# Moving modulation products from the latent attention's out projection to the even mixer behind it

## The chip, the core and the metric

The kernel runs on one NeuronCore of a Trainium2 chip. The metric is device time in microseconds (us), lower is better. It is the median of three runs, and one further execution was taken with a profiler that records every instruction of every engine. The engines are TensorE (PE, with its weight loads, PEld), VectorE (DVE), ScalarE (ACT), GpSimd (POOL) and SyncE (SP), which issues nearly all DMA transfers, in order, from one queue.

## The reference

Two transformer blocks of two layers each run over 256 latent and 256 context tokens of width 2048, all in float32. The mixers in order are a windowed attention, a latent attention (MLA), an "even" mixer (pooling, and a recurrence in both directions with 16 heads of 64) and an attention with grouped keys. Each layer is modulated by a condition vector:

```python
shift_l, scale_l, gate_l = jnp.split((sc @ mod_w[l] + mod_b[l])[:, None, :], 3, axis=-1)
hl = xl * (1.0 + scale_l) + shift_l
...
xl = layer_norm(DEEPNORM_ALPHA * xl + gate_l * yl, ln_g[l], ln_b[l])
```

`sc @ mod_w[l]` is a product of one row (two with the context's condition) by a 2048 x 6144 matrix. It depends on nothing but the inputs, so its place in the program is free as long as shift, scale and gate are there when a layer asks for them. There are four such matrices, 48 MB (MiB) each.

## The kernel before

Activations lie in SBUF with features on the partitions, as a rounded high part and a low rest (`hhi`, `hlo`). A dense layer streams its weights: `weights` loads two K-tiles (two times 128 rows, 512 columns) per DMA into a tile `raw`, `split` makes a high part `whi` (ACT, L323) and a low part `wlo` (DVE, L324), and PE makes three products for each block (`mm3`, L352 to L354). `weights` calls `fill()` once after each K-tile.

A modulation step (L260, in `mod_steps`) multiplies one 1 MB tile `mraw` of a modulation matrix (four K-tiles of 512 columns) by the condition. It is one row of the program on PE, "32x512 x4", and 8 records in the trace: four products on four column groups of the array. A batch of 16 steps ends with an ACT copy (L267) and four small products (L273). `fill` runs such steps at a rate per K-tile that is set anew for each of six stages by the table `PACE`:

```python
def fill(self):
    if self.mod_wait:
        self.mod_wait -= 1
        if not self.mod_wait and not self.mod_ahead:
            self.mod_load()
    for n in list(self.side):
        self.owed_side[n] = self.owed_side.get(n, 0.0) + self.side[n][1]
        steps = int(self.owed_side[n])
        self.owed_side[n] -= steps
        self.advance(n, steps)
```

`PACE` has the windowed attention, its out projection, the latent attention, its out projection, the even mixer, its out projection. Behind the last there is no modulation left. `mod_open` also gives a stage its number of `mraw` buffers: three in the out projections, one in the three mixers. `mod_load` issues the tile's DMA on SP. `need` runs the remaining steps of a group at once if a layer asks for one that isn't done.

The stage in question (L1757 to L1794) is the latent attention's out projection: four groups of 512 output columns, each of 16 K-tiles with 12 products of 256 columns, then the first weights of the even mixer (`ev_lora`, 2 times 16 K-tiles with 6 products each). A group ends with `residual` (DVE, L1471). Beside groups 1 to 3 and the first `ev_lora` pass run the puts (`put_h`) of the next layer's operands, two ACT and one DVE operation each. At the end the layer's result is stored (`xscratch`, L1793, 4 stores of 1 MB).

The even mixer (`even`, L945) runs 240 K-tiles of weights, with 512-column products, and beside them 16 units of the recurrence, up to four at a time, advanced by `fill` as well: long chains of small products on PE with DVE and ACT between them. `bon` (L1220) is one product of a unit that waits for a DVE operation (L1218). In this mixer `raw` has two buffers.

The order of instructions on each engine is set at build time, by a scheduler that puts instructions in order by when it thinks they are ready. The engines then run their queues in that order.

Of the kernel before, what the change touches and what calls it, by code (L numbers as in the profile page):

```python
# [36 lines left out]
ACTIVE = 4  # L37


PACE = 0.3, 0.5, 0.2, 0.5, 0.25, 0.5  # L40
MV_LAG = 1
MOD_LAG = 2
MEX = 1
# [73 lines left out]
class Net:  # L117
# [552 lines left out]
    def gqa(self, w, windowed, kb, v=None):  # L670
# [5 lines left out]
        with self.tc.tile_pool(name=pre, bufs=1) as ph:  # L676
# [28 lines left out]
            if windowed:  # L705
                self.mod_open(ph, 1, PACE[0])
            toks = range(q0 // P, 4)
# [75 lines left out]
    def mla(self, kvb):  # L783
        nc, I, h = self.nc, self.I, self.h
        scale = 192 ** -0.5
        with self.tc.tile_pool(name="mla", bufs=1) as ph:
# [39 lines left out]
            self.lin_tok(I["mla_in"][0], h, KD, 512, range(2, 4), ev_cq)  # L826
            self.mod_open(ph, 1, PACE[2])
            self.more(ph, MEX, RX[2], 2 * HG * P)
# [116 lines left out]
    def even(self, lb):  # L945
# [3 lines left out]
        with self.tc.tile_pool(name="ev", bufs=1) as ph:  # L949
            self.mod_open(ph, 1, PACE[4])  # L950
            if EX:
# [678 lines left out]
def tile_network(ctx, tc, I, out, dbg=None, stop=9):  # L1630
# [94 lines left out]
    with tc.tile_pool(name="x1", bufs=1) as px:  # L1725
        xn = px.tile([P, KD, NT], F32, name="x1")
        N.more(px, XX[0], RX[1])
        N.mod_open(px, 3, PACE[1])
        N.need(0, range(12))
# [28 lines left out]
    with tc.tile_pool(name="x2", bufs=1) as px:  # L1758
        xn = px.tile([P, KD, NT], F32, name="x2")
        N.more(px, XX[1], RX[3])  # L1760
        N.mod_open(px, 3, PACE[3])
        N.need(1, range(12))
# [37 lines left out]
    with tc.tile_pool(name="x3", bufs=1) as px:  # L1800
        xn = px.tile([P, KD, NT], F32, name="x3")
        N.more(px, XX[2], RX[5])
        N.mod_open(px, 3, PACE[5])
        N.need(2, range(12))
# [195 lines left out]
```

## Time and profile before

| what | value |
|---|---|
| median of 3 runs | 3386.61 us (3378.92 to 3392.72) |
| profiled execution, its own time | 3385.91 us |
| its span, first to last instruction | 3384.1 us |
| TensorE busy | 3198.0 us, 95% |
| weight loads busy (beside PE) | 2384.4 us, 70% |
| VectorE busy | 2051.4 us, 61% |
| ScalarE busy | 1541.6 us, 46% |
| modulation products (L260) busy | 234.0 us, 1536 records, 192 steps |
| mean granted TensorE clock | 0.978 |

PE is the busiest engine nearly everywhere. Busy time of PE counts overlapping products once, and the end of each is modelled, so a busy PE can still have room between the starts of its products. The stage of the change lies between 1356 and 1574 us of the span, the even mixer from there to about 2700, its out projection to about 2900.

### The profile page before, as it was taken

To read this page: it belongs to the slowest core of one execution; us is meant where nothing else is said; L and a number is where in the kernel's file an instruction comes from. 1 tells how busy PE (TensorE), PEld (TensorE's weight loads), DVE (VectorE), ACT (ScalarE), POOL (GpSimd) and SP (SyncE) were. 2 spreads that over 40 slices of the span, in tenths; PEclk is the share of its full clock that TensorE was granted. 3 is DMA by queue.
4 is the path that set the end of the run, shared out by engine and by line. 5 is a ranking of instruction groups with operands and counts; after the bars stand their busy time and mean duration, and the time that the engine had idled before them with its cause. 6 is when DMAs were issued, how large, how long until landed. Compare 5 with 4: busy or idle time off the path is not lost. (4 is left out here: it accounts for less than half of the span.)

```text
span 3384.1 us, 56050 instructions
## 1 busy us (share of the span) xinstructions
PE 3198.0 (95%) x21218; PEld 2384.4 (70%) x21218; DVE 2051.4 (61%) x4487; ACT 1541.6 (46%) x3461; POOL 195.8 (6%) x277
## 2 busy tenths in 40 slices
PE   5999999989989999898999989999999999899998
PEld 2567777767877777665766666666666678778887
DVE  2456455543476666442776676777777655867767
ACT  2424444442366655442344434444444433636654
POOL 0000000000001110000000000000000001200000
PEclk8999999999999999999999999999999999999999
DMA  7843444358654655988534222222323444544454
GB/s 299 307 161 126 144 140 144 131 198 292 213 166 155 212 193 194 369 340 320 170 119 125 76 76 79 73 73 66 99 80 93 133 168 131 174 129 144 132 174 157
DMA packets 270784, 556.27 MB, mean 164 GB/s; under 512 B 122928, under 2 KB 150704, under 8 KB 244912
## 3 DMA queue, kind: packets, MB, share of 16 engines
q1 hardware_dynamic: 270512, 552.68, 49.0%
q8 instruction: 167, 2.74, 0.3%
q14 instruction: 105, 0.86, 0.1%
HBM read 517.46 MB, written 35.13 MB: 163 GB/s over the span
## 5 line engine op out<-in xcount | busy, mean ns | idle before, releaser
L324 DVE TENSOR_TENSOR wlo<-raw,whi 128x512 fp32r<-128x512 f32 (+2 forms) x1000 | 658.7, 668 | 610.4 <-ACT whi L323 573.3
L352 PE MATMUL a<-hhi,whi 128*128 128x512 f32 (+1 forms) x2752 | 975.9, 357 | 32.6 <-ACT whi L323 29.6
L323 ACT CAST whi<-raw 128x512 fp32r<-128x512 f32 (+2 forms) x1000 | 591.8, 599 | 865.1 <-PE a L353 448.9
L353 PE MATMUL a<-hlo,whi 128*128 128x512 f32 (+1 forms) x2752 | 950.5, 347 | 0.2 <-DVE hlo L445 0.2
L354 PE MATMUL a<-hhi,wlo 128*128 128x512 f32 (+1 forms) x2752 | 938.6, 349 | 5.6 <-DVE wlo L324 5.1
L352 PEld LDWEIGHTS a<-hhi,whi 128*128 128x128 f32 x2752 | 524.3, 191 | 192.9 <-ACT whi L323 79.6
L354 PEld LDWEIGHTS a<-hhi,wlo 128*128 128x128 f32 x2752 | 518.5, 191 | 72.5 <-DVE wlo L324 14.1
L353 PEld LDWEIGHTS a<-hlo,whi 128*128 128x128 f32 x2752 | 525.3, 191 | 54.2 <-issue 3.0
L352 PE MATMUL a<-whi,hhi 128*128 128x512 f32 (+1 forms) x672 | 262.8, 401 | 16.1 <-ACT sq L613 5.9
L353 PE MATMUL a<-wlo,hhi 128*128 128x512 f32 (+1 forms) x672 | 264.5, 394 | 0.3
L456 POOL TENSOR_TENSOR rs<-st,mhalf 128x4 f32<-128x4 f32 (+3 forms) x109 | 140.9, 1293 | 2097.5 <-DVE st L453 1910.8
L354 PE MATMUL a<-whi,hlo 128*128 128x512 f32 (+1 forms) x672 | 260.4, 390 | 0.0
L260 PE MATMUL mv<-mraw,cs 128*32 128x512 f32 x1536 | 234.0, 632 | 21.4 <-DMA mraw<-mod_w 21.3
L352 PEld LDWEIGHTS a<-whi,hhi 128*128 128x128 f32 x672 | 127.1, 191 | 74.2 <-issue 22.2
L353 PEld LDWEIGHTS a<-wlo,hhi 128*128 128x128 f32 x672 | 128.9, 192 | 30.0 <-DVE wlo L324 5.4
L354 PEld LDWEIGHTS a<-whi,hlo 128*128 128x128 f32 x672 | 128.9, 192 | 26.0 <-issue 1.1
L565 ACT ACTIVATE pr<-sc,nm 128x512 f32<-128x512 f32 (+1 forms) x128 | 81.0, 632 | 93.3 <-DVE nm L562 62.6
L1385 ACT ACTIVATE SD<-SV,DL 64x64 f32<-64x64 f32 x224 | 77.2, 345 | 63.3 <-DVE SV L1399 60.1
L556 DVE TENSOR_REDUCE mx<-sc 128x1 f32<-128x512 f32 (+1 forms) x128 | 78.9, 617 | 40.3 <-PE sc L354 23.4
L1399 DVE SCALAR_TENSOR_TENSOR SV<-chain,DL,SD 64x64 f32<-64x64 f32 x224 | 63.3, 283 | 59.7 <-PE chain L1393 51.6
L572 ACT ACTIVATE pr<-pr,rc 128x512 f32<-128x512 f32 (+1 forms) x128 | 85.6, 669 | 22.0 <-DVE rc L571 21.9
L260 PEld LDWEIGHTS mv<-mraw,cs 128*32 128x32 f32 x1536 | 33.9, 110 | 85.1 <-issue 38.6
(371 smaller groups left out, 4465.9 us busy)
## 6 DMA issues: line engine op xcount, KB each, us to landing
mraw<-mod_w SPq DMA_DIRECT2D x192, 1024.0 KB, 5.0
raw<-od_in SPq DMA_DIRECT2D x88, 512.0 KB, 3.5
raw<-swa_in SPq DMA_DIRECT2D x72, 512.0 KB, 3.6
raw<-ev_rkv SPq DMA_DIRECT2D x64, 384.0 KB, 3.5
raw<-ev_in SPq DMA_DIRECT2D x48, 512.0 KB, 3.6
raw<-swa_out SPq DMA_DIRECT2D x40, 512.0 KB, 5.6
raw<-ev_out SPq DMA_DIRECT2D x40, 512.0 KB, 3.4
raw<-mla_g SPq DMA_DIRECT2D x64, 256.0 KB, 3.1
```

What stands on the lines that cost most here:

```text
L260: nc.tensor.matmul(pb[32 * j : 32 * j + 32, :], cs[:, 32 * k + 30 - 2 * n : 32 * k + 62 - 2 * n], raw[:, j, :], start=(n == 0 and q == 0), ...
L323: nc.scalar.copy(whi, raw)
L324: nc.vector.tensor_tensor(wlo, raw, whi.bitcast(F32), op=ALU.subtract)
L352: mm(out, ah, bh, start=first, stop=False, skip_group_check=shared)
L353: mm(out, ah, bl, start=False, stop=False, skip_group_check=shared)
L354: mm(out, al, bh, start=False, stop=last, skip_group_check=shared)
L456: self.nc.gpsimd.tensor_tensor(dst, stv, mv, op=ALU.pow)
L556: nc.vector.reduce_max(mx, sc, axis=AX.X)
L565: nc.scalar.activation(pr[:, :n], sc, AF.Exp, scale=scale, bias=nm, accum_out=sm)
L572: nc.scalar.activation(pr[:, :n], pr[:, :n], AF.Copy, scale=rc)
L1385: nc.scalar.activation(SD[r_], SV[r_, hh, c, :], AF.Copy, scale=DL[r_, c : c + 1])
L1399: nc.vector.scalar_tensor_tensor(SV[r_, hh, c + 1, :], ps[r_, 128:192], DL[r_, c : c + 1], SD[r_], ALU.mult, ALU.add)
```

## The change

One number of the table: the rate of modulation steps beside the latent attention's out projection becomes 0.

```diff
-PACE = 0.3, 0.5, 0.2, 0.5, 0.25, 0.5
+PACE = 0.3, 0.5, 0.2, 0, 0.25, 0.5
```

On PE, in group 1 of the projection (a_13503 to a_13506, the accumulators of one group before, a_13455 to a_13458 now), a modulation step stood behind every second K-tile. Before:

```order
L353 MATMUL a_13506<-hlo,whi_13755 128x256
L354 MATMUL a_13506<-hhi,wlo_13756 128x256
L260 MATMUL mv_13896<-mraw_13749,cs_9274 32x512 x4
L352 MATMUL a_13503<-hhi,whi_13777 128x256
L353 MATMUL a_13503<-hlo,whi_13777 128x256
```

and now:

```order
L353 MATMUL a_13458<-hlo,whi_13481 128x256
L354 MATMUL a_13458<-hhi,wlo_13482 128x256
L352 MATMUL a_13455<-hhi,whi_13503 128x256
L353 MATMUL a_13455<-hlo,whi_13503 128x256
L354 MATMUL a_13455<-hhi,wlo_13504 128x256
```

The step is gone and the K-tiles follow each other. In all, 45 of the 192 steps leave this stage, 3 stay at its start.

On SP, at the end of the stage, the last weights of `ev_lora` and the first of the even mixer (`ev_rkv`) stood beside modulation tiles, with the four stores of the result between them. Before:

```order
L240 DMA mraw_14989<-mod_w 128x2048
L338 DMA raw_15001<-ev_lora 128x512
L240 DMA mraw_15013<-mod_w 128x2048
L1793 DMA xscratch<-x_13094 128x2048 x4
L338 DMA raw_15048<-ev_rkv 128x768
L338 DMA raw_15082<-ev_rkv 128x768
L240 DMA mraw_15063<-mod_w 128x2048
```

and now:

```order
L338 DMA raw_14521<-ev_lora 128x512
L1793 DMA xscratch<-x_13094 128x2048
L338 DMA raw_14539<-ev_lora 128x512
...
L338 DMA raw_14701<-ev_lora 128x512
L338 DMA raw_14719<-ev_lora 128x512
L338 DMA raw_14760<-ev_rkv 128x768
L338 DMA raw_14794<-ev_rkv 128x768
L240 DMA mraw_14775<-mod_w 128x2048
```

The last store stands eleven loads ahead of the even mixer's first weights, the three others earlier still, and no modulation tile lies between them.

On PE in the even mixer (the seventh chunk of the recurrence's sixth unit, `chain`), before:

```order
L354 MATMUL a_19495<-hhi,wlo_19915 128x512
L1404 MATMUL chain_19587<-SV_19089,QB_18892 64x64 x2
L352 MATMUL a_19496<-hhi,whi_19914 128x512
L353 MATMUL a_19496<-hlo,whi_19914 128x512
L354 MATMUL a_19496<-hhi,wlo_19915 128x512
L1376 MATMUL chain_19587<-SV_19089,AQ_18678 64x64 x2
```

and now:

```order
L1404 MATMUL chain_19324<-SV_18814,QB_18611 64x64 x2
L353 MATMUL a_19229<-hlo,whi_19728 128x512
L354 MATMUL a_19229<-hhi,wlo_19729 128x512
L260 MATMUL mv_17136<-mraw_19629,cs_9274 32x512
L1376 MATMUL chain_19324<-SV_18814,AQ_18391 64x64 x2
L260 MATMUL mv_17136<-mraw_19629,cs_9274 32x512 x3
```

A modulation step has come in, and the scheduler has cut it in two around a product of the recurrence. The even mixer had 16 steps and 4 such cuts; it now has 51 steps and 22 cuts. Its out projection had no step and has 10, with one cut.

## Rows read from the trace of the kernel before

**Rows 1.** Stretch, its us, busy PE PEld DVE ACT POOL (records), clock, DMA share, GB/s.
```profile
1356.30:1404.80 48.50, 37.76 (x253) 27.26 (x250) 18.63 (x39) 19.49 (x44) 0.00 (x0) 0.86 1.00 379
1404.80:1438.10 33.30, 32.52 (x258) 25.45 (x258) 15.01 (x33) 16.56 (x35) 0.00 (x0) 1.00 0.94 364
1438.10:1471.20 33.10, 33.01 (x251) 24.92 (x251) 12.64 (x23) 11.18 (x22) 0.00 (x0) 1.00 0.96 373
1471.20:1507.50 36.30, 32.89 (x258) 24.70 (x257) 16.88 (x32) 17.58 (x36) 0.00 (x0) 1.00 0.96 360
1507.50:1562.00 54.50, 49.69 (x321) 30.32 (x320) 14.28 (x28) 13.36 (x25) 0.00 (x0) 0.94 0.87 341
1562.00:1573.60 11.60, 1.09 (x10) 0.17 (x9) 1.67 (x6) 1.55 (x4) 1.46 (x13) 0.64 0.92 363
```

**Rows 2.** PE in time order, one period of group 1 (start, length, instruction, count).
```profile
1409.86 1.07 PE L260 MATMUL mv<-mraw,cs 128*32 128x512 f32 x8
...
1413.92 0.64 PE L260 MATMUL mv<-mraw,cs 128*32 128x512 f32 x4
```

**Rows 3.** PE in time order: the last layer's out projection begins.
```profile
3266.09 0.74 PE L352 MATMUL a<-hhi,whi 128*128 128x256 f32 x4 [1.17 <-ACT hhi L444]
```

**Rows 4.** DVE in time order: `residual` ends groups 0 and 1 of that projection.
```profile
3294.92 1.66 DVE L1471 SCALAR_TENSOR_TENSOR x<-a,mod,res 128x256 f32<-128x256 f32 x4 [0.58 <-PE a L354]
...
3318.60 1.66 DVE L1471 SCALAR_TENSOR_TENSOR x<-a,mod,res 128x256 f32<-128x256 f32 x4 [0.58 <-PE a L354]
```

**Rows 5.** ACT by line and form, groups 1 to 3 (1404 to 1507).
```profile
L323 ACT CAST whi<-raw 128x512 fp32r<-128x512 f32 x48 | 27.2, 616 | 32.4 <-DMA raw<-mla_out 23.9 <-PE a L353 4.1 <-PE mv L260 3.2
L494 ACT ACTIVATE hf<-x,mod,s 128x256 f32<-128x256 f32 x22 | 12.6, 598 | 4.6 <-DVE hlo L500 4.6
L498 ACT CAST hhi<-hf 128x256 fp32r<-128x256 f32 x23 | 8.8, 404 | 10.6 <-PE a L354 10.6
```

**Rows 6.** PE's waits, 1560 to 1578 (in total, times, longest).
```profile
PE a L352 <- ACT whi L323: 10.7, 2, 10.5
```

**Rows 7.** Busy time in two stretches of 24 K-tiles each in the even mixer.
```profile
1688.50:1822.30 133.80, 132.63 (x1109) 86.93 (x1108) 92.27 (x211) 56.91 (x154) 9.88 (x21) 1.00 0.37 114
1965.80:2095.30 129.50, 125.51 (x1061) 86.55 (x1060) 92.87 (x212) 56.90 (x155) 9.07 (x17) 0.99 0.27 72
```

**Rows 8.** PE's waits: first in 1688.5 to 1822.3, then in 1965.8 to 2095.3.
```profile
PE bon L1220 <- DVE r L1218: 0.9, 1, 0.9
...
PE bon L1220 <- DVE r L1218: 4.0, 1, 4.0
```

**Rows 9.** PE in time order: a cut step in the even mixer.
```profile
1812.10 1.05 PE L260 MATMUL mv<-mraw,cs 128*32 128x512 f32 x2
1813.07 1.20 PE L354 MATMUL a<-hhi,wlo 128*128 128x512 f32 x4
1814.20 1.06 PE L260 MATMUL mv<-mraw,cs 128*32 128x512 f32 x6
1815.19 0.98 PE L1430 MATMUL yt<-ident,y 128*128 128x128 f32 x7
```

**Rows 10.** Busy time: even mixer without steps, its out projection, the last out projection.
```profile
1890.00:2690.00 800.00, 769.89 (x6491) 526.54 (x6491) 583.44 (x1332) 358.33 (x965) 54.69 (x97) 0.98 0.31 85
2806.00:2850.00 44.00, 44.00 (x196) 36.45 (x195) 20.76 (x35) 12.27 (x20) 5.83 (x4) 1.00 0.35 110
3295.00:3318.00 23.00, 23.00 (x194) 23.00 (x194) 18.97 (x42) 11.58 (x23) 0.00 (x0) 1.00 0.72 221
```

**Rows 11.** PE's waits in the even mixer without steps (1890 to 2690), the longest one.
```profile
PE bon L1220 <- DVE r L1218: 16.2, 6, 5.4
```

**Rows 12.** SP's waits in the even mixer with steps (1600 to 1890).
```profile
SPq L240 <- PE mv L260: 51.9, 10, 11.0
```

**Rows 13.** The page, DMA issues (KB each, us to landing).
```profile
raw<-ev_rkv SPq DMA_DIRECT2D x64, 384.0 KB, 3.5
raw<-mla_out SPq DMA_DIRECT2D x32, 512.0 KB, 8.1
```

## The prediction

> **What bounds the kernel now.** I read the busy time by stretch first, because one share over the whole span mixes stages with different limits. In the six stretches of the stage that changes [rows 1] the DMA engines are busy 87 to 100% of the time and move 341 to 379 GB/s, while TensorE (PE) is busy 38 of 48 us in group 0 and 33 of 36 in group 3. The granted clock is 0.86 in group 0 and 0.64 in the last stretch, that is, a part of each runs at 1.2 GHz, behind the waits, where the rest has 2.4. So the stage has two limits: PE where the products stand close, the DMA engines elsewhere. The same shape of work without modulation is in the trace: the last layer's out projection, whose groups keep PE busy 23.0 of 23.0 us at 221 GB/s and a clock of 1.00 [rows 10]. A weight tile of 512 KB lands 8.1 us after its issue in our stage, where one of 384 KB in the even mixer takes 3.5 [rows 13], and ScalarE (ACT) spends 23.9 us of three groups idle until a weight tile lands [rows 5]. The reader is to see in this that a modulation step costs twice: once on PE, and once as a megabyte that stands before the weights.
>
> The even mixer has the opposite face. Its DMA share is 0.31 and it moves 85 GB/s; PE is busy 770 of 800 us [rows 10]. What PE waits for longest is VectorE (DVE), at the product `bon` of the recurrence: 16.2 us in 6 waits [rows 11].
>
> **The change part by part.** Moved are 45 steps: 35 go to the even mixer, 10 to its out projection.
>
> *A step on PE.* In group 1 two K-tiles and a step take 1413.92 - 1409.86 = 4.06 us [rows 2]. Two K-tiles alone take (3318.60 - 3294.92) / 8 = 2.96 us in the last out projection [rows 4]. A step costs 1.1 us where PE is full.
>
> *What the stage loses.* Groups 1 and 2: from 33.3 and 33.1 us [rows 1] to 23.7 each [rows 4]; ACT has room for it (16 casts at 0.616, 8 puts at 0.598 + 0.404, together 17.9 us [rows 5]). Saved: 9.6 + 9.4 = 19.0.
> Group 0: its twin, also with operands that come back from memory, takes 3294.92 - 3266.09 = 28.8 us [rows 3, 4]. One step stays (1.1), and I add 3 us because that step's tile still has to land before PE goes on: 33, from 48.5. Saved: 15.5 (19.7 if it is as its twin).
> Group 3: 12 of its 16 K-tiles have a put beside them, on ACT 0.616 + 0.598 + 0.404 = 1.6 us against PE's 1.48 a K-tile. So 12 x 1.62 + 4 x 1.48 = 25.3 us; I take 26, from 36.3. Saved: 10.3.
> `ev_lora`: 192 products, as many as a group has, so 23.7 at best; with four puts at its start I take 26, from 54.5. It is the richest stretch because its 32 K-tiles had only 6 products each, and the steps' megabytes stood against so little PE time. Saved: 28.5.
> The wait behind it: PE stands 10.5 us until the even mixer's first weights are converted [rows 6]. Ahead of them in the queue now stand 4 MB of stores and modulation tiles; afterwards one store at most, eleven loads before. I leave 3 of the 11.6 us. Saved: 8.6.
> Together 15.5 + 19.0 + 10.3 + 28.5 + 8.6 = 82 us. From below: if the waits stay and only PE work goes, 45 x 1.1 = 50. From above: group 0 as its twin, group 3 and `ev_lora` at 23.7, no wait: 94.
>
> *What the even mixer pays.* Two of its stretches of 24 K-tiles hold the same instructions, one with modulation steps and one without: 1109 and 1061 PE records, 48 or six steps apart, DVE 211 and 212 [rows 7]. They take 133.8 and 129.5 us. Six steps cost 4.3 us, 0.72 each, two of the six being cut. The saving against the full price lies in `bon`: PE waits 4.0 us there without the steps and 0.9 with them [rows 8], because PE comes later to a VectorE that is behind. Without that, (4.3 + 3.1) / 6 = 1.23 a step. For 35 steps these ends give 25 and 43 us; I take 1.0, 35 us, since there are 16.2 us of such waits to meet in 800 us [rows 11] but a step every four K-tiles will not meet them all. A cut step keeps PE for 1813.07 - 1812.10 = 0.97 us with its first quarter and for 1815.19 - 1814.20 = 0.99 with the rest [rows 9]: a cut costs a step's time once more, about 1.0. At two in six, 51 steps would have 17 cuts; the new order has 22. Five more: 5 us. The even mixer pays 40. If PE is full throughout, it pays 35 x 1.1 + 18 x 1.0 = 57; if the better pair is the rule and the cuts cost nothing more, 25.
>
> *What its out projection pays.* A group keeps PE busy 44.0 of 44.0 us, with 110 GB/s [rows 10]: no room on PE, much on DMA. 10 x 1.1 and one cut: 12 us.
>
> *The queues.* The 35 loads in the even mixer enter SP's queue ahead of weights and of the recurrence's small transfers, with one buffer: each load waits until the step before has run on PE. SP stood 51.9 us so in ten waits already [rows 12], which PE did not feel: in the stretch with six steps it waits 0.9 us at `bon` and for no weight tile worth a row [rows 8]. I cost this at nothing; it is a rival below. ACT and DVE lose nothing but three batches' copies, which only change their place.
>
> The sum: -82 + 40 + 12 = -30 us, on the span of 3384.1 us and on the execution's 3385.9. The median of the runs is 0.7 us above that, so 3386.6 - 30 = 3357.
>
> **The rivals.**
> *Full price.* PE is 96% busy in the even mixer, and the pair of stretches was a lucky one: 4.0 of the 16.2 us stood in it. Then -82 + 57 + 12 = -13: 3373 us, not to be told from no change. Against it: three quarters of the waits lie elsewhere and are there to be met too.
> *The stage keeps its waits.* Group 3's long waits might come from the puts, not from DMA, and `ev_lora` might be held by conversion. Then it is -50 + 52: 3389. Against it: ACT is busy 17.6 of 36.3 us in group 3 [rows 1], and its idle time ends on landings [rows 5].
> *Slower: the single buffer.* SP's longest wait for a step was 11.0 us [rows 12]; whatever weight tile stands behind it is late, and the even mixer has only two raw tiles. If every second of the 35 steps makes PE wait for one landing, 3.5 us [rows 13], that is 60 us on top of the full price: -13 + 60 = +47, 3433. It decides from 30 us on, 0.9 us for each moved step. Against it are the waits of the stretch with steps [rows 8].
> *The mixer has room.* Weight loads fill 527 of 800 us in the even mixer, 66%, where the last out projection has 23.0 of 23.0 [rows 10]. If a third of PE's time were really free there, the steps would fall into it, with the cuts between chain products hidden as well: some 10 us for all of them, -82 + 10 + 12 = -60, 3327. Against it: the six steps did cost 4.3 us [rows 7].
> The Trainium skill (Perfetto Trace Analysis, Identifying the Most-Contended Engine) says that matmul busy time is no measure of the room on TensorE and that weight-load busy time is one. By that rule this last rival holds; the trace bears it out in part, since a step cost 0.72 there and not 1.1.
>
> **How the numbers follow.** The forecast, 3357, has 0.58; full price 0.17; the stage keeps its waits 0.09; slower 0.08; room 0.08. The forecast's own bounds (94 and 50 saved, 25 and 57 paid) and the rivals at 3373 and 3327 give 3330 to 3386, which leaves the slower case and half of the waits' case out. A measurement of this kernel can tell about 0.5%, 17 us. Faster by more than that: nearly all of the forecast, the room, a part of full price: 0.68. Within: 0.23. Slower: 0.09.
>
> **What would show it.** In the new profile groups 1 and 2 should end 23 to 24 us apart, `ev_lora` should take 23 to 30, DMA fall to about 200 GB/s there, and the wait ahead of the even mixer to under 5 us. The waits at `bon` should shrink from 16 us. The prediction is wrong if the even mixer grows by over 57 us, if PE waits there for `whi` behind modulation loads, or if the stage saves under 60.

## The result and the profile after

The changed kernel takes 3359.84 us (median of 4 runs, 3357.37 to 3361.96) where the kernel before, run beside it, takes 3387.21 (3378.92 to 3392.72): a ratio of 0.9928, 95% interval 0.9911 to 0.9944, 27 us. The forecast was 3357. The profiled span went from 3384.1 to 3358.6 us, and its mean granted clock from 0.978 to 0.984.

The first view of after is again busy time by stretch: groups 0 to 3, the `ev_lora` passes, then the even mixer with the first group of its out projection, and the rest of that projection. The columns are those of [rows 1].

```profile
1356.30:1387.40 31.10, 25.42 (x189) 23.27 (x190) 16.56 (x34) 19.18 (x43) 0.00 (x0) 0.89 0.95 331
1387.40:1411.00 23.60, 23.51 (x194) 23.20 (x194) 17.55 (x34) 19.43 (x42) 0.00 (x0) 1.00 0.80 274
1411.00:1434.10 23.10, 23.10 (x195) 23.10 (x195) 12.50 (x21) 9.88 (x17) 0.00 (x0) 1.00 0.70 251
1434.10:1457.10 23.00, 23.00 (x194) 23.00 (x193) 16.62 (x33) 17.48 (x37) 0.00 (x0) 1.00 0.61 205
1457.10:1481.40 24.30, 24.15 (x201) 23.95 (x200) 13.07 (x25) 12.32 (x25) 1.09 (x10) 1.00 0.64 207
...
1481.40:2720.30 1238.90, 1215.74 (x9392) 794.00 (x9391) 834.65 (x1880) 512.78 (x1345) 77.67 (x148) 0.99 0.41 129
2720.30:2875.20 154.90, 149.75 (x869) 120.97 (x867) 89.67 (x165) 57.36 (x103) 24.59 (x23) 0.99 0.57 198
```

The last two stretches of the kernel before, cut at the same instructions:

```profile
1573.60:2765.80 1192.20, 1156.46 (x9110) 788.66 (x9111) 834.36 (x1873) 509.64 (x1344) 77.47 (x144) 0.98 0.36 104
2765.80:2901.40 135.60, 133.86 (x780) 118.36 (x778) 88.69 (x161) 56.80 (x102) 24.57 (x23) 1.00 0.48 151
```

The stage now looks as the last out projection did [rows 10]: PE busy from end to end and a clock of 1.00 behind group 0. The table above and [rows 1] both begin at 1356.30. The stage's first product stands there before, and 0.86 us earlier now:

```profile
1356.33 0.74 PE L352 MATMUL a<-hhi,whi 128*128 128x256 f32 x4
```

```profile
1355.47 0.74 PE L352 MATMUL a<-hhi,whi 128*128 128x256 f32 x4
```

Counted from it, the stage took 217.3 us and takes 125.9. The wait of 11.6 us behind it is gone: the last `ev_lora` product and the mixer's first product of 512 columns stand 0.11 us apart.

```profile
1481.30 0.28 PE L354 MATMUL a<-hhi,wlo 128*128 128x256 f32 x1
1481.41 0.40 PE L352 MATMUL a<-hhi,whi 128*128 128x512 f32 x1
```

So the span's 25.5 us are made up of: 0.9 ahead of the stage, the stage -91.3, the mixer 1238.9 - 1192.2 = +46.7, its out projection 154.9 - 135.6 = +19.3, and about 0.7 lost behind it. In the mixer PE has 1215.74 - 1156.46 = 59.3 us more busy time and 12.6 us less idle time (23.2 where it had 35.7).

The clock column moved too, and it hides a part of the mixer's price. Added up over the trace's record of the clock, the mixer of before stood 36 us at 1.2 GHz, the changed one 17. At half the clock work takes up to twice its time, so at most 18 and 9 us were lost by it: up to some 9 us of the steps' price were given back by the clock (an estimate from these two sums).

### The profile page after: what moved, and what is told of

The parts are those of the page before. It is cut to its first block, busy times and chain, and to the rows that moved or that the text cites. A ratio compares the mean times of both kernels' runs of the same rounds, so it can differ in the third digit from the quotient of the medians.

```text
span 3358.6 us, 56061 instructions
## 1 busy us (share of the span) xinstructions
PE 3206.8 (95%) x21218; PEld 2374.5 (71%) x21218; DVE 2050.3 (61%) x4487; ACT 1543.9 (46%) x3461; POOL 195.4 (6%) x277
## 4 chain that ended last, share of the span: by engine, by line
PE 80%; DVE 8%; DMA 4%; ACT 3%; issue 2%; POOL 2%; SPq 0%; POOLq 0%; DVEq 0%; ACTq 0%
PE a L352 19%; PE a L354 17%; PE a L353 17%; PE mv L260 6%; PE gram L1241 2%; DMA mraw<-mod_w 2%; POOL rs L456 2%; PE ptr L591 1%; PE sc L352 1%; DVE wlo L324 1%; PE chain L1376 1%; PE chain L1380 1%; PE inv L1341 1%; PE chain L1388 1%; ACT whi L323 1%
## 5 line engine op out<-in xcount | busy, mean ns | idle before, releaser
L260 PE MATMUL mv<-mraw,cs 128*32 128x512 f32 x1536 | 251.0, 634 | 19.5 <-DMA mraw<-mod_w 19.2
L260 PEld LDWEIGHTS mv<-mraw,cs 128*32 128x32 f32 x1536 | 36.1, 110 | 93.0 <-issue 52.2
```

Source lines behind the costliest of these rows:

```text
L260: nc.tensor.matmul(pb[32 * j : 32 * j + 32, :], cs[:, 32 * k + 30 - 2 * n : 32 * k + 62 - 2 * n], raw[:, j, :], start=(n == 0 and q == 0), ...
```

## The experiments

The questions were: is the stage's part the bytes or the products; what of the mixer's 46.7 us are the steps and what the cuts; why do ten steps cost 19 us in the out projection; and is there a better place. Each kernel was run beside the kernel before, which had medians between 3383.5 and 3385.5. e1_loads, e2_products, e8_none and e11_out_025 have one execution each. Kernels reach the stage at different times, so its lengths below are counted from its first product.

**e1_loads and e2_products: bytes or products.** Both start from the kernel before; `slim` is true within the stage alone, and only the lines that act are shown. In the first most products of the stage go, in the second its loads:

```diff
-                        for j in range(4):
+                        ends = n == 0 and q == 0 or n == len(gs) - 1 and q == 3
+                        for j in range(1 if self.slim and not ends else 4):
```

```diff
+            raw = self.kept
+            if raw is None:
+                raw = pool.tile([P, 4, 512], F32, tag="mraw", name=self.nm("mraw"), bufs=bufs)
+                self.nc.sync.dma_start(out=raw, in_=self.I["mod_w"][i, g, q])
+            if self.slim:
+                self.kept = raw
```

> The kernel before with the stage's modulation loads kept and most of its products taken away: 41 of its steps keep one product of four (the modulation values of these batches are therefore not the reference's). The stage took 217.3 us before and moved 78.7 MB, 363 GB/s on the mean. If the DMA engines set the stage's length, the bytes are the same and it still takes 195 to 215 us, the program 3365 to 3385. If PE's work sets it, a step gives back most of its 1.1 us and the weights land in time: the stage takes about 180 us or less, the program under 3350.

> The kernel before with the stage's modulation products kept and its loads taken away: all steps of the stage multiply one tile that is loaded once (the modulation values of these steps are not the reference's). If half of what a step costs in the stage is its megabyte, the stage takes the 125 us of the changed kernel plus 45 x 1.1 = 50, 170 to 185 us, and the program about 3345. If the bytes cost nothing, the stage keeps its 217 us and the program its 3386.

They took 3376.9 and 3350.1 us. Busy time by stretch, e1_loads (group 1 and the `ev_lora` passes with the wait behind them), then e2_products (the same stretches):

```profile
1402.80:1435.60 32.80, 32.02 (x229) 25.52 (x228) 14.60 (x32) 17.32 (x38) 0.00 (x0) 1.00 0.95 374
...
1503.70:1566.00 62.30, 46.90 (x236) 28.66 (x236) 14.60 (x32) 14.17 (x28) 1.46 (x13) 0.91 0.91 361
sum 209.70, PE 180.50 PEld 129.58 DVE 77.28 ACT 78.61 POOL 1.46; mean PE 36.10 PEld 25.92 DVE 15.46 ACT 15.72 POOL 0.29
```

```profile
1396.80:1429.00 32.20, 32.20 (x251) 25.39 (x250) 14.20 (x29) 15.19 (x30) 0.00 (x0) 1.00 0.55 187
...
1495.10:1536.30 41.20, 41.20 (x319) 26.66 (x318) 12.02 (x25) 11.90 (x23) 0.00 (x0) 1.00 0.37 114
sum 180.00, PE 173.76 PEld 125.86 DVE 78.38 ACT 80.54 POOL 0.00; mean PE 34.75 PEld 25.17 DVE 15.68 ACT 16.11 POOL 0.00
```

Counted from its first product (at 1353.17 and 1354.42), the stage keeps 212.9 of its 217.3 us in e1_loads, and takes 181.9 in e2_products. e2_products decides: with all products and no bytes PE is busy nearly throughout (173.8 of the 180.0 us in the windows), and the stage still takes 181.9 - 125.9 = 56 us more than without steps. So of the 91 us the products cost some 56, and the bytes, with the waits that they bring, the other 35. Up to 11 of the 35 are clock: the stage stood 29 us at 1.2 GHz before and 7 in e2_products. e1_loads decides nothing between the two, although its stage kept its length: a single product keeps PE nearly as long as four do (below), so it kept PE's work as well as the bytes (180.5 us busy, 187.0 before).

**e4_some and e7_groups: a few steps back.** If bytes set the end, a few steps should be cheap in a stage that now moves 205 to 274 GB/s behind group 0.

```diff
-PACE = 0.3, 0.5, 0.2, 0, 0.25, 0.5
+PACE = 0.3, 0.5, 0.2, 0.2, 0.25, 0.5
```

> The changed kernel with some steps back in the stage: rate 0.2 instead of 0, some 16 steps, fewer in the mixer and its out projection. Taking a step out of the stage gave back 92 / 45 = 2.0 us on the mean, and the mixer and its out projection paid 1.4 and 1.9. If the stage's cost is DMA time beyond PE time, the first 16 steps find the DMA engines free (125 us hold 45 MB at 363 GB/s, the stage without steps moves some 32), cost 1.1 us each there and give back 1.4 to 1.9: 8 to 12 us faster than the change, about 3349. If each step costs its mean of 2.0 us there, it is 0 to 10 us slower than the change, about 3365.

It took 3367.36 us (0.9946, interval 0.9930 to 0.9963), 7 slower than the change; the second answer held. The stage took 160.5 us. The four groups paid 20 us for 12 steps (16 if one counts from 1356.3, but this kernel begins the stage at 1351.73); the `ev_lora` passes took 37.8 us with 6 steps where they took 23.1 with none (both from the last operation of group 3 on):

```profile
1474.40:1512.20 37.80, 36.09 (x247) 25.79 (x246) 13.87 (x31) 12.56 (x25) 1.46 (x13) 1.00 0.85 309
```

The second kernel stops the steps there:

```diff
-        lb = [N.acc() for _ in range(2)]
+        lb = [N.acc() for _ in range(2)]; N.pace(0)
```

> The run at rate 0.2 in the stage with the rate at 0 from its last weights (the ev_lora passes) on. In that run the four groups paid 16 us for 12 steps and the ev_lora passes 14.7 for 6, 2.45 each, since a K-tile has 6 products there and not 12. If that is the reason, the ev_lora passes come back to within 3 us of 23.1, the stage takes 138 to 144 us, and the program 3352 to 3361. If the price of a step there has nothing to do with the passes (it is the stores or the end of the stage), the stage stays above 150.

The passes came back to 25.8 us with one step left, but the stage took 149.9 us (146.4 from 1356.3), and the program 3362.25 (3355.65 to 3368.65): no better than the change. The reason in mind, that 6 products a K-tile leave too little PE time for a megabyte to land in, is not what the rows of e4_some show. In its passes PE is busy 36.1 of 37.8 us, where it is busy 22.95 of 23.10 without steps: 13 of the 14.7 us are work and under 2 are waits. The trace shows that the scheduler had cut the six steps there five times, so eleven pieces ran, at 1.2 us each. In the groups one of the 12 steps was cut, and PE waited some 4 us more than without them. Where PE is full from end to end, room on the DMA engines is no room for a step.

**e3_whole and e5_follow: what a cut costs.** In the profile of after, PE in time order shows a cut step: one product, a product of the recurrence, the other three.

```profile
1817.63 1.04 PE L260 MATMUL mv<-mraw,cs 128*32 128x512 f32 x2
1818.60 0.33 PE L1404 MATMUL chain<-SV,QB 64*64 64x64 f32 x4
1818.86 1.06 PE L260 MATMUL mv<-mraw,cs 128*32 128x512 f32 x6
1819.85 0.55 PE L1274 MATMUL vt<-ident,v 128*128 128x128 f32 x3
```

The first piece keeps PE 0.97 us and the second 0.99. The first attempt gave all four products a priority over everything:

```diff
-                            nc.tensor.matmul(
+                            with self.tc.high_priority(offset=4000): nc.tensor.matmul(
```

> The changed kernel with every modulation step in one piece: its four products get a priority that nothing else has, so the scheduler puts no product of the recurrence between them. 227 pieces become 192. If a cut costs a step's time once more, 1.0 us each, the program is 35 us shorter, about 3325. If a cut costs nothing beyond what the recurrence's product would have waited for otherwise, it stays within 10 us of 3360. If the recurrence needs the cuts (a whole step keeps its product waiting for up to 1.1 us), it is longer, up to 25 us.

It took 3378.86 us, 19 more than the change; the stage's first product came 16 us later (at 1371.2), and the mixer took 1239.4 us for 1238.9. Taken alone this said that cuts are free. The waits of PE say otherwise: in the mixer, and then in all that lies ahead of the stage, PE stood at steps whose tile had not landed (in the changed kernel 1.0 us in the mixer, 13.8 us ahead of the stage).

```profile
PE bon L1220 <- DVE r L1218: 16.2, 7, 4.1
PE mv L260 <- DMA mraw<-mod_w: 7.4, 5, 2.6
```

```profile
PE mv L260 <- DMA mraw<-mod_w: 31.1, 24, 3.8
```

The edit had moved the steps as well as joined them: the scheduler puts a step of top priority where it thinks that the tile has landed, and the chip lands it later. The mixer lost in waits and by the clock what it gained in pieces: idle time is 34.0 us where after has 23.2, and it stood 41 us at 1.2 GHz where after stood 17, which takes up to 12; busy time, with that in it, fell only from 1215.7 to 1205.4. So the next kernel leaves the first product where it stood:

```diff
-                            nc.tensor.matmul(
+                            with self.tc.high_priority(offset=4000) if j else ExitStack(): nc.tensor.matmul(
```

> The changed kernel with uncut steps again, but each step's first product stands where it stood: only its other three products have the priority, so they follow at once and no step runs ahead of its tile. 35 pieces fewer, all else in place. If a cut costs the program the 0.98 us that each piece keeps PE, it is 35 us shorter, about 3325, the even mixer 22 us shorter. If the mixer's length is set by the recurrence's chain as much as by PE, the freed time comes back as waits ahead of the chain's products, and it stays within 8 us of 3360.

3326.62 us (3325.10 to 3327.74; 0.9830, interval 0.9815 to 0.9844): 33 us faster than the change, for 35 pieces fewer. The whole step, and the mixer's window, in e5_follow:

```profile
1809.11 1.06 PE L260 MATMUL mv<-mraw,cs 128*32 128x512 f32 x8
1810.11 0.33 PE L1404 MATMUL chain<-SV,QB 64*64 64x64 f32 x4
```

```profile
1472.00:2688.00 1216.00, 1192.49 (x9391) 790.37 (x9391) 835.38 (x1876) 513.27 (x1345) 76.59 (x148) 1.00 0.42 132
```

Four products side by side take 1.00 us, one takes 0.97: a cut costs a whole step's time. The mixer is 22.9 us shorter for 22 cuts, all of it busy time (23.2 us); the idle time stays at 23.5. Up to 3 of the 23 us are clock (10 us at 1.2 GHz where after has 17), so a cut is worth 0.9 to 1.05 us. The other 10 us were gained ahead of the stage, where 12 cuts went too: its first product stands 10 us earlier. The Trainium skill (TensorEngine Tiling (Array Packing), Key Properties) says that column tiles run in parallel and that a change of the tiling drains TensorE; these rows agree with the first. No run here shows the second: that a piece of one product takes the time of four follows from the first alone.

**e9_follow_before: the change without cuts.** The same line in the kernel before.

> The kernel before with the same uncut steps: the stage keeps its 48. 19 pieces fewer than before (211 to 192), so at 1.0 us a cut 3386 - 19 = 3367, and without cuts the change is worth 3367 - 3326.6 = 40 us where it is worth 27 with them: the difference are the 16 cuts that it adds. If the uncut steps help the changed kernel by something else than their number, the kernel before gains as much as the changed one, 33 us: 3353.

3372.47 us (0.9963, interval 0.9948 to 0.9979): 12 us gained, at most 18 by the interval, and not the 33 of the second answer. Without cuts the change is worth 3372.5 - 3326.6 = 46 us, with them 27: the cuts that it adds ate some 19 us of it, where their number says 16. The size is loose, give or take 9 us by the intervals of the three comparisons together (an estimate).

**e8_none: the mixer without steps.**

```diff
-PACE = 0.3, 0.5, 0.2, 0.5, 0.25, 0.5
+PACE = 0.3, 0.5, 0.2, 0.5, 0, 0.5
```

> The kernel before with no step in the even mixer; its 16 steps there run in its out projection (the stage as before). The mixer took 1192.2 us up to the end of the first group of the out projection with 17 steps and 1238.9 with 51, 1.37 us a step. If a step there has one price, the mixer without steps takes 1192 - 17 x 1.37 = 1169. If its first steps fall into waits and only the later ones cost, it takes 1185 or more. The out projection pays the 16 steps at 1.1 to 1.9, 18 to 30 us.

3428.0 us. The out projection paid some 20 us, as expected, but for the mixer neither number was right: it took 1214.9 us with one step, 23 more than with 17. The whole window, the worst part of it, and within that a wait of PE and the stretch that begins with it:

```profile
1571.80:2786.70 1214.90, 1171.63 (x8966) 804.15 (x8967) 832.36 (x1859) 510.68 (x1341) 79.79 (x144) 0.96 0.31 88
```

```profile
2161.30:2266.90 105.60, 100.72 (x716) 65.36 (x714) 63.59 (x157) 43.60 (x123) 6.99 (x14) 0.84 0.22 58
```

```profile
2202.50 1.19 PE L1220 MATMUL bon<-r,c_bones 128*128 128x512 f32 x1 [4.20 <-DVE r L1218]
```

```profile
2201.00:2235.00 34.00, 32.50 (x158) 22.34 (x158) 17.29 (x38) 8.00 (x20) 0.10 (x1) 0.50 0.17 46
```

PE stood 4.2 us at `bon`, the clock fell to 1.2 GHz, and it stayed there for 34 us although PE was busy 32.5 of them. Over the whole window PE's idle time is 43.3 us, against 35.7 before and 23.2 after, and the mixer stood 100 us at 1.2 GHz, against 36 before and 17 after: at most 50 us lost, where before lost 18. So some 23 us less of steps and cuts came with up to 32 us of clock and 8 of waits. That makes up to 17 of the 23 us; the order of the recurrence moved too, and what made the rest stays open. Among these three kernels more steps in the mixer go with a higher clock and fewer waits, but one execution of each is too little for a rule: e3_whole, with 51 steps that waited for their tiles, stood 41 us at 1.2 GHz. No term of the prediction had the clock.

**e6_all_mixer, e10_follow_030, e12_follow_mla: other places for the last ten steps.** The out projection's ten steps go into the mixer (rate 0.35; rate 0.3 with uncut steps) or into the latent attention (rate 0.27, uncut).

```diff
-PACE = 0.3, 0.5, 0.2, 0, 0.25, 0.5
+PACE = 0.3, 0.5, 0.2, 0, 0.35, 0.5
```

> The changed kernel with the even mixer's rate at 0.35 instead of 0.25: the ten steps of its out projection come into the mixer too. The out projection took 154.8 us with ten steps and 135.6 with none, so it gives back 19 us. The mixer paid 1.37 us a step for the moved ones: 10 to 14 us more if that holds, 5 if a further step costs what the last eight of the run at rate 0.2 did (0.6 each). So 3346 to 3355. If the single tile buffer makes weights late at this rate, the mixer pays over 19 us and the program is above 3360.

> The changed kernel with uncut steps and the mixer's rate at 0.3: most of the out projection's ten steps come into the mixer. The out projection gives back 12 to 19 us, the mixer pays 0.8 us for each uncut step (34 of them cost 1216.1 - 1192.2 + 4 cuts = 28 us): 3316 to 3322. If at the higher rate the steps wait for their tile again, as at 0.35 (10.5 us in six waits), it stays at 3326.

> The changed kernel with uncut steps and the latent attention's rate at 0.27 instead of 0.2: it takes some ten to twelve steps more, the out projection of the even mixer none. The out projection gives back 17 to 19 us; the latent attention pays 1.1 us for each step if PE is full there, 11 to 13: 3318 to 3322 against 3326.6. If its steps wait for their tile, as the mixer's did at rate 0.3 (6.1 us in three waits), nothing is left of it: 3325 to 3330.

They took 3360.55, 3329.73 and 3333.89 us (3326.92 to 3338.59). The out projection gave back its 17 to 19 us each time, and it was spent at once: the mixer went to 1254.8 us (from 1238.9), and uncut to 1237.6 (from 1216.0). In e12_follow_mla 15 steps more than in e5_follow run ahead of the mixer (146 for 131), and it begins 32 us later; it gives back 11 us for five steps fewer. What PE waits for in the three, first the mixer at 0.35 and at 0.3, then the latent attention:

```profile
PE mv L260 <- DMA mraw<-mod_w: 10.5, 6, 2.5
```

```profile
PE mv L260 <- DMA mraw<-mod_w: 6.1, 3, 3.0
```

```profile
PE mv L260 <- DMA mraw<-mod_w: 8.6, 13, 1.8
```

With one tile buffer, a rate above what ran before makes the steps themselves late: this wait is 1.0 us in the changed kernel's mixer, 2.1 in that of e5_follow, and 5.2 in the latent attention window of e5_follow. It is not all of the price. In e10_follow_030 the mixer also stood 31 us at 1.2 GHz where e5_follow stood 10, up to 10 us of its 21.6. None of the three is faster than e5_follow; e10_follow_030 is within the noise of it.

**e11_out_025: the out projection.** After its first steps PE in time order reads, in the changed kernel:

```profile
2726.34 1.07 PE L260 MATMUL mv<-mraw,cs 128*32 128x512 f32 x8
2730.82 0.50 PE L352 MATMUL a<-hhi,whi 128*128 128x512 f32 x1 [3.42 <-ACT whi L323]
2731.16 0.39 PE L353 MATMUL a<-hlo,whi 128*128 128x512 f32 x1
2731.39 0.50 PE L352 MATMUL a<-hhi,whi 128*128 128x512 f32 x1
...
2732.55 0.63 PE L353 MATMUL a<-hlo,whi 128*128 128x512 f32 x1
2732.97 0.63 PE L352 MATMUL a<-hhi,whi 128*128 128x512 f32 x1
```

A weight tile is late behind the modulation loads, and then the products start 0.42 us apart where they start 0.23 apart at full clock: 1.2 GHz, the lower of the two levels.

```diff
-PACE = 0.3, 0.5, 0.2, 0, 0.25, 0.5
+PACE = 0.3, 0.5, 0.2, 0, 0.25, 0.25
```

> The changed kernel with the rate in the even mixer's out projection at 0.25 instead of 0.5. The ten steps cost 19.2 us there: three of them stood in the first 6 us, and PE then waited 3.5 us for a weight tile behind their loads and went on at half clock for 3 us. If the bunch is the reason, the out projection takes 146 to 149 us instead of 154.8, and the program is 6 to 9 us shorter, 3352. If a step costs 1.9 us there wherever it stands, it stays at 154 and 3360.

3362.1 us, and 158 us in the out projection. But the bunch had not gone: the first three steps stood within 7 us of its begin, much as they had before. So the run does not test the reason, and nothing is shown beyond the rows above: ten steps and a cut at 1.1 and 1.0 make 12; the wait of 3.4, and some 3 us at the lower clock, which cost about half their length, lead to 17 of the 19.

## Why the prediction was right

**The stage: 82 forecast, 91 measured.** Groups 1 and 2 ended as the twin of [rows 4] said, 23.6 and 23.1 us. Group 0 took 31.9 from its first product up to its `residual` for 33. The rest was too careful: group 3 took 23.0 and not 26, with ACT 17.5 us busy beside it: the puts, which I had put on the path, lay beside PE's work; `ev_lora` took 24.3 for 26; the wait behind it nothing for 3. The upper bound (94) was close. That a step costs twice in this stage, on PE and as a megabyte, is shown by e2_products, 56 and 35 us of the 91. "The stage keeps its waits" fell: it had 50 for the saving.

**The mixer: 40 forecast, 46.7 measured.** Here errors partly cancel. The price on PE was set too low: busy time grew by 59.3 us, of which 18 cuts more at 23.2 / 22 = 1.05 are 19 and 34 steps (the window has 51 by the trace, for 17) 1.19 each, 40. That is a floor, since the clock gave back up to 9 us; without that a step cost up to 1.5. The step that failed is "I take 1.0", which leans on a pair of stretches at 0.72 a step, with two cuts in six steps; and the added cuts were counted as 5 beyond that share. The reading of the pair left out the clock column of [rows 7]: the stretch without steps has 0.99, by the record 3.4 us at 1.2 GHz, so up to 1.7 us of its length are clock, and the six steps cost up to 6.0 us and not 4.3. The rival at full price had 57 for the same thing and was near on PE, again with the clock left out. But it left out, too, that steps meet waits: PE's idle time fell by 12.6 us, where the forecast needed 17 (57 - 40). PE's longest wait in the changed mixer:

```profile
PE bon L1220 <- DVE r L1218: 12.8, 8, 3.7
```

The same stretch had 17.1 before: 4 us fewer. The other waits that shrank are those ahead of the recurrence's inversion (`inv` and `z`, 9.4 us in six waits before, 3.1 in three now).

**The out projection: 12 forecast, 19.3 measured.** The term had PE's work alone. The late weight tile and the lower clock behind it were not in it, and the rows show them in this place; that they are the cause of the whole difference is not shown, as e11_out_025 did not remove them.

**The queues: nothing forecast, nothing measured.** SP's wait for a step went from 51.9 us in ten waits [rows 12] to

```profile
SPq L240 <- PE mv L260: 209.8, 39, 15.9
```

and yet PE waits for `whi` in the mixer 1.5 us in all. The slower rival, the single buffer, did not come at this rate; it begins at the rates of e6_all_mixer and e10_follow_030, as late steps and not as late weights.

**The mixer has room** fell: it asked for 10 us, and 46.7 were paid. By the rule named there from the Trainium skill (Perfetto Trace Analysis, Identifying the Most-Contended Engine), weight loads at 66% meant room; in this trace the busy time was the better guide, since 59.3 us more of it made 46.7 us of time.

So the sum, -82 + 40 + 12 = -30, was -91 + 47 + 19 = -25 in the span: each term was too small, and the errors of the givers and the takers nearly cancelled. That the mechanism and the signs were right is the prediction's merit; that 3357 lies 3 us from 3360 is in part luck, for the single terms are off by 7 to 9. The range's upper end, 3386, does not follow from the bounds named for it: 50 saved against 57 and 12 paid gives 3405.

## What to carry to other kernels

A step that brings both bytes and products was worth moving out of a stage whose DMA engines are busy nearly all the time; the gain is the products plus the bytes that PE's work didn't cover, minus what the new place asks. There, price it by busy time and count the pieces into which a scheduler cuts it: products that run side by side in the array cost their whole time once more for each cut, and holding them together was worth more here (33 us) than the move (27). When an edit that should help does not, look whether it moved the work as well as changed it, and what the clock did: compare the clock column of both stretches before you call their difference the price of an instruction.

## What the runs showed of the hardware

Four modulation products on four column groups take PE 1.00 us, three 0.99 and one 0.97.

The granted clock of one part differs between kernels that change little in it, and between runs of one kernel: the mixer had 0.96 with one step, 0.98 with 17, 0.99 with 51, 1.00 with 51 uncut, and 0.98 with 51 that waited for their tiles (e3_whole). In e8_none it stayed at 0.50 for 34 us behind a wait of PE of 4.2 us, with PE busy 32.5 of the 34. The seven runs of e9_follow_before lay between 3362.6 us at a mean clock of 0.981 and 3379.8 at 0.975, those of e5_follow at 0.984 to 0.987 within 2.6 us.
